# Modulation vectors: four groups' partial products folded before the one-hot matmuls

## The chip, the cores and the metric

The kernel runs on one core of a Trainium2 chip. The metric is the device time of one execution in microseconds (us). Before the change the median of three runs is 1930.26 us (1930.08 to 1930.78). The profiled execution took 1928.32 us, of which 1926.5 us lie between its first and last instruction (the span).

## The reference, cut to what matters

Two transformer blocks of two layers each run over 256 tokens of width 1024, in float32. The part that the change touches is the modulation of the second block: for each of its two layers a vector of 6144 numbers is made from one conditioning vector `c` of 1024 numbers.

```
c_act = jax.nn.silu(c)
for l in range(2):
    mod = c_act @ w_ada[l] + b_ada[l]          # (1024,) @ (1024, 6144)
    sh1, sc1, g1, sh2, sc2, g2 = split(mod, 6)
    h  = rms_norm(x, ln1_g[l]) * (1 + sc1) + sh1
    ...
```

The two `w_ada` matrices are 48 MB of float32 weights, against one row of activations. All else (feed-forward networks, gated linear attention, attention, pooling) is the same before and after.

## The kernel before, in words

**Streaming.** All weights are read once, as chunks of about 1 MB that SyncE (SP) loads into four `raw` buffers. A chunk is cut into units of 128 columns. ScalarE rounds a unit into `uhi` (line 169), VectorE makes the rest `ulo = raw - uhi` (line 170), and TensorE does three matmuls for each block of 128 rows: high by high, high by low, low by high. This splitting runs five units ahead of TensorE. A step of the stream is one unit's matmuls, or those of a few units.

**The modulation.** `ada_plan` cuts each layer's `w_ada` into 24 groups of 256 columns, and `ada_job` puts one group's 1 MB chunk into the stream. The 48 jobs stand in the first block's four feed-forward networks, twelve in each: four between its gate and up projections, eight between its down projections. A job is VectorE's: one TENSOR_SCALAR (line 641) and seven SCALAR_TENSOR_TENSORs (line 639) multiply the chunk's eight row blocks by columns of `cact` and add them up in `acc`, 128 partitions by 256. What is left is the sum over the 128 partitions. For it GpSimd (POOL) rounds `acc` into `ah` (line 648) and makes the rest `al` (line 649), and TensorE multiplies both by a one-hot matrix, a slice of `hot`: row `i` of twelve in the PSUM tile `pso` gets the column sums of group `i`, the other rows get zeros. So each group of columns costs two matmuls of 256 columns.

**When they run.** `rest()` is put off to the end of the next step (`st.lag`). From there `st.later_pe(6, pe)` counts six further steps; then the two one-hot matmuls go into `st.small`, and `unit_mm` and `unit_two` take one of them out before each row block's matmuls. After twelve groups `ada_out` copies the rows out of PSUM (line 670), turns them with two transposes (line 675) and adds the bias.

**Buffers.** `tmp` tiles share eleven buffers of a row of 272, `slot` tiles share sixteen of 4 x 272; whoever writes a reused buffer waits for its last reader. The rings of both pools run through all parts of the kernel: `acc`, `ah` and `al` are `tmp` tiles, as are the results of the feed-forward networks' evictions on VectorE (lines 716 and 728). `pso` is one PSUM buffer, which no one else uses in a feed-forward network. A scheduler orders each engine's instructions from the recorded order and from what they wait for. POOL does little else: it sets tiles to zero, issues two small loads of `gla_w2` for each mixer of the first block (line 1225) and one of the positions (line 583), and adds shifted rows in the pooling of the second block (line 1513).

Of the kernel before, what the change touches and what calls it, by code (L numbers as in the profile page):

```python
# [10 lines left out]
F32 = mybir.dt.float32  # L11
F32R = mybir.dt.float32r
# [3 lines left out]
ALU = mybir.AluOpType  # L16
# [260 lines left out]
def two_block_kernel(ctx: ExitStack, tc: tile.TileContext, I, cst, msk, out, dbg=None, stop=None):  # L277
    nc = tc.nc
    V, S, P, G = nc.vector, nc.scalar, nc.tensor, nc.gpsimd

    const = ctx.enter_context(tc.tile_pool(name="const", bufs=1))
# [24 lines left out]
    def ps_o():  # L306
        return pso.tile([128, 512], F32, name="pso", tag="pso")
# [7 lines left out]
    def tmp(n=T1, dt=F32):  # L315
        return tmp_p.tile([128, n], dt, name="tmp", tag="tmp")

    def slot(k, n, dt=F32):
        return slot_p.tile([128, k, n], dt, name="slot", tag="slot")
# [8 lines left out]
    st = Stream(nc, raw_p, un_p)  # L328
# [22 lines left out]
    identr, negr = qmt[:, 0, :], qmt[:, 1, :]  # L351
    vmt = const.tile([128, 128], F32R, name="vmt")
    ptm = const.tile([128, 256], F32R, name="ptm")
    hot = const.tile([128, 24], F32R, name="hot")
    modT = const.tile([128, 2, 48], F32, name="modT")
    mder = const.tile([128, 2, 40], F32, name="mder")

# [10 lines left out]
    def mm(ps, lhsT, rhs, start, stop):  # L368
        P.matmul(ps, lhsT=lhsT, rhs=rhs, start=start, stop=stop)  # L369
# [152 lines left out]
    def cols(dst, src, n):  # L522
        ps = ps_t()
        P.transpose(ps[:, 0:n], src[0:n, :], ident[0:n, 0:n])
        S.copy(out=dst[:, 0:n], in_=ps[:, 0:n])
# [37 lines left out]
    def set_up():  # L563
        ra, rb, rc = consts["r"]
        cols(colA, ra, 80)
        cols(colB, rb, 122)
        cols(colC, rc, 20)
        S.activation(out=bmh, in_=colA[:, A_BM:A_BM + 32], func=AF.Copy, scale=0.5)
        S.activation(out=gnh, in_=colA[:, A_GN:A_GN + 8], func=AF.Copy, scale=0.5)
        for l in range(2):  # L570
            S.activation(out=gq8[:, l:l + 1], in_=colC[:, C_QK + 2 * l:C_QK + 2 * l + 1], func=AF.Copy, scale=0.125)
        hf = tmp(24)
        G.memset(hf, 0.0)
        G.memset(hf[:, 12:13], 1.0)
        S.copy(out=hot, in_=hf)
        cth = tmp(8)
        S.activation(out=cth, in_=colC[:, C_C:C_C + 8], func=AF.Tanh, scale=0.5)
        V.scalar_tensor_tensor(out=cth, in0=cth, scalar=1.0, in1=colC[:, C_C:C_C + 8], op0=ALU.add, op1=ALU.mult)
        V.tensor_scalar(out=cact, in0=cth, scalar1=0.5, scalar2=None, op0=ALU.mult)
# [40 lines left out]
    ada = {}  # L620
# [7 lines left out]
    def ada_job():  # L628
        if not ada_q:
            return  # L630
        l, j, src = ada_q.pop(0)
        ch = Chunk(src, 8, 256)

        def fn(t):
            acc = tmp(256)

            def part(k0, k1):
                for k in range(k0, k1):
                    V.scalar_tensor_tensor(out=acc, in0=t[:, k, :], scalar=cact[:, k:k + 1], in1=acc, op0=ALU.mult, op1=ALU.add)  # L639

            V.tensor_scalar(out=acc, in0=t[:, 0, :], scalar1=cact[:, 0:1], scalar2=None, op0=ALU.mult)
            part(1, 4)

            def rest():
                part(4, 8)
                ah = tmp(256, F32R)
                al = tmp(256, F32R)
                G.tensor_copy(out=ah, in_=acc)
                G.tensor_tensor(out=al, in0=acc, in1=ah.bitcast(F32), op=ALU.subtract)
                i = j % 12  # L650

                def one(x, first, last):
                    if first:
                        ada["p"] = ps_o()
                    mm(ada["p"][0:12, 0:256], hot[:, 12 - i:24 - i], x, first, last)
                    if last:
                        st.lag(lambda: ada_out(l, j - 11))

                def pe():
                    st.small.append(lambda: one(ah, i == 0, False))  # L660
                    st.small.append(lambda: one(al, False, i == 11))
                st.later_pe(6, pe)
            st.lag(rest)

        st.job(ch, fn)

    def ada_out(l, j0):

        rows = tmp(256)
        S.copy(out=rows[0:12], in_=ada["p"][0:12, 0:256])  # L670

        def turn():
            ps = ps_t()
            for i in range(2):
                P.transpose(ps[:, 12 * i:12 * i + 12], rows[0:12, 128 * i:128 * i + 128], ident[0:12, 0:12])
            c0 = 2 * j0
            V.tensor_tensor(out=modT[:, l, c0:c0 + 24].rearrange("p (j i) -> p j i", i=2), in0=ps[:, 0:24].rearrange("p (i j) -> p j i", i=2),
                            in1=colB[:, B_AD + 48 * l + c0:B_AD + 48 * l + c0 + 24].rearrange("p (j i) -> p j i", i=2), op=ALU.add)
        st.later_pe(2, turn)
# [1060 lines left out]
    if True:  # L1740
# [14 lines left out]
        for l in range(2):  # L1755
            for part in range(3):
# [9 lines left out]
                if l == part == 0:  # L1766
                    st.after_mm(lambda: st.later_pe(6, set_up))
# [90 lines left out]
```

## Time and profile before

| | |
|---|---|
| median of three runs | 1930.26 us |
| the profiled execution, whole | 1928.32 us |
| its span | 1926.5 us |
| TensorE busy (matmul) | 1899.2 us, 99% |
| VectorE busy | 1551.7 us, 81% |
| ScalarE busy | 1078.3 us, 56% |
| GpSimd busy | 110.1 us, 6% |
| moved by DMA | 364 MB, mean 189 GB/s |

Names as the profile has them: PE is TensorE's matmuls, PEld its weight loads, DVE is VectorE, ACT is ScalarE, POOL is GpSimd, SP is SyncE. A row `out<-in` names what an instruction writes and reads, and L369 is line 369 of the kernel, the helper through which nearly all matmuls go. A PE row's duration of some 0.28 us includes the time in the pipeline; matmuls follow each other sooner, so what one costs is read from the start of one row to the start of the next. Granted TensorE clock was 0.996 of full speed (2.4 GHz) over the span.

### The profile page before, as it was taken

What the parts mean: (1) busy time and instruction counts of PE and PEld (TensorE: products, weight loads), DVE (VectorE), ACT (ScalarE), POOL (GpSimd) and SP (SyncE); (2) the same over time, 40 slices, a digit from 0 to 9 for tenths busy, and PEclk for the clock granted to TensorE, in tenths of its full rate; (3) what the DMA queues carried; (4) which work ended last, traced back from release to release, by engine and by line L of the source; (5) the groups of instructions that cost most, each with busy time, mean ns of one, the idle gap of its engine ahead of it and who ended that gap; (6) DMA issues with size and microseconds to landing.
All of it is one profiled execution on the core that took longest, in us unless ns stands there. A gap on an engine that the chain in (4) does not pass through costs nothing.

```text
span 1926.5 us, 35869 instructions
## 1 busy us (share of the span) xinstructions
PE 1899.2 (99%) x14386; PEld 1821.9 (95%) x14386; DVE 1551.7 (81%) x2932; ACT 1078.3 (56%) x1883; POOL 110.1 (6%) x146
## 2 busy tenths in 40 slices
PE   9999999999999999999999999999999999999998
PEld 8999989899999999998999999899999889999987
DVE  6978888887889887888888898986888557788854
ACT  5444456755444544456666455577676447767642
POOL 1001100000001100110000010120000002000000
PEclk9999999999999999999999999999999999999999
DMA  7767742356659766874236686944665554456551
GB/s 239 242 214 260 238 154 67 88 175 197 219 192 297 231 213 211 271 237 132 88 92 209 195 267 227 290 130 156 190 189 191 181 169 134 159 186 190 194 176 66
DMA packets 349715, 364.00 MB, mean 189 GB/s; under 512 B 6138, under 2 KB 339516, under 8 KB 349548
## 3 DMA queue, kind: packets, MB, share of 16 engines
q1 hardware_dynamic: 349372, 361.51, 58.4%
q8 instruction: 113, 1.85, 0.4%
q14 instruction: 54, 0.44, 0.1%
q0 software_dynamic: 176, 0.20, 0.0%
HBM read 360.64 MB, written 1.05 MB: 188 GB/s over the span
## 4 chain that ended last, share of the span: by engine, by line
PE 86%; DVE 7%; ACT 4%; issue 1%; DMA 1%; SPq 0%; DVEq 0%; ACTq 0%
PE big L369 38%; PE pss L369 23%; PE pst L369 20%; PE pso L369 3%; DVE ulo L170 2%; ACT uhi L169 1%; PE pst L1474 0%; PE pst L1172 0%; DMA raw<-in_w_in_dram 0%; DVE slot L928 0%; DVE tmp L639 0%; DVE tmp L1297 0%; DVE slot L1359 0%; DVE slot L926 0%; ACT tmp L1137 0%
## 5 line engine op out<-in xcount | busy, mean ns | idle before, releaser
L169 ACT CAST uhi<-raw 128x1024 fp32r<-128x1024 f32 (+3 forms) x642 | 622.3, 975 | 618.1 <-PE big L369 251.5
L170 DVE TENSOR_TENSOR ulo<-raw,uhi 128x1024 fp32r<-128x1024 f32 (+3 forms) x644 | 731.7, 1140 | 186.8 <-ACT uhi L169 179.5
L369 PE MATMUL big<-xh,uhi 128*128 128x272 f32 (+2 forms) x1560 | 453.7, 291 | 0.9 <-DVE slot L876 0.9
L369 PE MATMUL big<-xl,uhi 128*128 128x272 f32 (+2 forms) x1560 | 446.9, 286 | 0.8 <-DVE xl L1648 0.8
L369 PE MATMUL big<-xh,ulo 128*128 128x272 f32 (+2 forms) x1560 | 446.9, 286 | 0.0
L369 PEld LDWEIGHTS big<-xh,uhi 128*128 128x128 f32 x1560 | 296.2, 190 | 5.8 <-issue 4.0
L369 PEld LDWEIGHTS big<-xl,uhi 128*128 128x128 f32 x1560 | 296.3, 190 | 1.7 <-DVE xl L1648 1.0
L369 PEld LDWEIGHTS big<-xh,ulo 128*128 128x128 f32 x1560 | 296.0, 190 | 0.1
L369 PE MATMUL big<-slot,uhi 128*128 128x272 f32 (+2 forms) x1224 | 287.8, 317 | 0.0
L369 PE MATMUL big<-slot,ulo 128*128 128x256 f32 (+1 forms) x781 | 221.5, 284 | 0.5 <-DVE ulo L170 0.5
L369 PEld LDWEIGHTS big<-slot,uhi 128*128 128x128 f32 x1224 | 202.1, 189 | 16.3 <-ACT uhi L169 0.2
L369 PE MATMUL pss<-slot,uhi 128*128 128x272 f32 (+2 forms) x814 | 195.2, 319 | 0.3 <-ACT P L1460 0.3
L369 PE MATMUL pst<-xh,uhi 128*128 128x272 f32 (+2 forms) x672 | 191.5, 287 | 0.0
L369 PE MATMUL pss<-xh,uhi 128*128 128x272 f32 (+2 forms) x664 | 190.2, 289 | 0.7 <-DVE h L512 0.7
L369 PE MATMUL pst<-xh,ulo 128*128 128x272 f32 (+2 forms) x672 | 190.9, 286 | 0.0
L369 PE MATMUL pst<-xl,uhi 128*128 128x272 f32 (+2 forms) x672 | 190.7, 286 | 0.0
L369 PE MATMUL pss<-xl,uhi 128*128 128x272 f32 (+2 forms) x664 | 189.0, 287 | 0.0
L369 PE MATMUL pss<-xh,ulo 128*128 128x272 f32 (+2 forms) x664 | 188.4, 286 | 0.0
L369 PE MATMUL pst<-slot,uhi 128*128 128x272 f32 (+2 forms) x730 | 177.9, 322 | 0.0
L639 DVE SCALAR_TENSOR_TENSOR tmp<-raw,cact,tmp 128x256 f32<-128x256 f32 x336 | 164.5, 489 | 3.5
L369 PE MATMUL pss<-slot,ulo 128*128 128x256 f32 (+1 forms) x525 | 148.9, 284 | 0.0
L369 PEld LDWEIGHTS big<-slot,ulo 128*128 128x128 f32 x781 | 147.6, 189 | 0.7 <-DVE ulo L170 0.7
(451 smaller groups left out, 3209.6 us busy)
## 6 DMA issues: line engine op xcount, KB each, us to landing
raw<-in_w_ff_dram SPq DMA_DIRECT2D x64, 1024.0 KB
raw<-in_w_in_dram SPq DMA_DIRECT2D x60, 1024.0 KB
raw<-in_w_ada_dram SPq DMA_DIRECT2D x48, 1024.0 KB
raw<-in_ffn_w_up_dram SPq DMA_DIRECT2D x44, 1024.0 KB
raw<-in_ffn_w_gate_dram SPq DMA_DIRECT2D x43, 1024.0 KB
raw<-in_ffn_w_down_dram SPq DMA_DIRECT2D x32, 1024.0 KB
raw<-in_w_out_dram SPq DMA_DIRECT2D x16, 1024.0 KB
raw<-in_ffn_w_down_dram SPq DMA_DIRECT2D x16, 768.0 KB
```

The lines of the kernel that those rows point to most:

```text
L169: nc.scalar.copy(out=hi[:, k], in_=src[:, k])
L170: self.lag(lambda k=k: nc.vector.tensor_tensor(out=lo[:, k], in0=src[:, k], in1=hi[:, k].bitcast(F32), op=ALU.subtract))
L369: P.matmul(ps, lhsT=lhsT, rhs=rhs, start=start, stop=stop)
L639: V.scalar_tensor_tensor(out=acc, in0=t[:, k, :], scalar=cact[:, k:k + 1], in1=acc, op0=ALU.mult, op1=ALU.add)
```

## The change

Four jobs in a row now form a set. After each job POOL issues four DMAs, which copy the four 32-partition quarters of `acc` side by side into partitions 32q to 32q+31 of a `slot` tile `b`, where q is the job's place in its set. After the fourth job POOL adds the four quarters of `b` (two TENSOR_TENSORs, over 512 and 256 columns), so that 32 partitions are left to sum for each group, and makes `ah` and `al` of the result once for the set. `hot` has a 1 in column 8+q for the 32 rows of place q, so one pair of one-hot matmuls gives four rows of `pso`. Three pairs fill the twelve rows, where there were twelve pairs. The pair is put into `st.small` eight steps after the fourth job instead of six after every job.

```diff
-    hot = const.tile([128, 24], F32R, name="hot")
+    hot = const.tile([128, 20], F32R, name="hot")
...
-        hf = tmp(24)
+        hf = tmp(20)
         G.memset(hf, 0.0)
-        G.memset(hf[:, 12:13], 1.0)
+        for q in range(4):
+            G.memset(hf[32 * q:32 * q + 32, 8 + q:9 + q], 1.0)
...
             def rest():
                 part(4, 8)
+                q, i = j % 4, j // 4 % 3
+                if q == 0:
+                    ada["b"] = slot(4, 256)
+                b = ada["b"]
+                for a in range(4):
+                    G.dma_start(out=b[32 * q:32 * q + 32, a, :], in_=acc[32 * a:32 * a + 32])
+                if q < 3:
+                    return
                 ah = tmp(256, F32R)
                 al = tmp(256, F32R)
-                G.tensor_copy(out=ah, in_=acc)
-                G.tensor_tensor(out=al, in0=acc, in1=ah.bitcast(F32), op=ALU.subtract)
-                i = j % 12
+                G.tensor_tensor(out=b[:, 0:2, :], in0=b[:, 0:2, :], in1=b[:, 2:4, :], op=ALU.add)
+                G.tensor_tensor(out=b[:, 0, :], in0=b[:, 0, :], in1=b[:, 1, :], op=ALU.add)
+                G.tensor_copy(out=ah, in_=b[:, 0, :])
+                G.tensor_tensor(out=al, in0=b[:, 0, :], in1=ah.bitcast(F32), op=ALU.subtract)

                 def one(x, first, last):
                     if first:
                         ada["p"] = ps_o()
-                    mm(ada["p"][0:12, 0:256], hot[:, 12 - i:24 - i], x, first, last)
+                    mm(ada["p"][0:12, 0:256], hot[:, 8 - 4 * i:20 - 4 * i], x, first, last)
...
-                    st.small.append(lambda: one(al, False, i == 11))
-                st.later_pe(6, pe)
+                    st.small.append(lambda: one(al, False, i == 2))
+                st.later_pe(8, pe)
```

How the built programs differ at three places. First POOL, from the set-up of `hot` to the first mixer's loads of `gla_w2`; before, a CAST and a TENSOR_TENSOR stand there for each of the first four jobs.

```order
L573 MEMSET tmp 128x24
L574 MEMSET tmp 128x1
L648 CAST tmp<-tmp 128x256
L649 TENSOR_TENSOR tmp<-tmp 128x256
...
L1223 MEMSET slot 32x512
L1225 DMA slot<-in_gla_w_dram 16x4x64 x2
```

In the changed kernel a set of four jobs is sixteen DMAs and four instructions, two sets stand ahead of the mixer's MEMSET, and four DMAs of the third.

```order
L573 MEMSET tmp 128x20
L575 MEMSET tmp 32x1 x4
L652 DMA slot<-tmp 32x256 x16
L657 TENSOR_TENSOR slot<-slot 128x512
L658 TENSOR_TENSOR slot<-slot 128x256
L659 CAST tmp<-slot 128x256
L660 TENSOR_TENSOR tmp<-slot,tmp 128x256
...
L652 DMA slot<-tmp 32x256 x4
L1233 MEMSET slot 32x512
L1235 DMA slot<-in_gla_w_dram 16x4x64 x2
```

So the loads of `gla_w2` have moved from behind the fourth job to behind the ninth. Over the whole program POOL gets 192 of the DMAs and 12 of each of the four instructions, and loses its 48 pairs.

Second PE, in the down projections of the last feed-forward network. The names with numbers are single tiles; before, the pair of job 43 (counted from 0) stands round the first matmuls of the unit `uhi_14836`, and the next two units are `uhi_14862` and `uhi_14912`.

```order
L369 MATMUL pso_13388<-tmp_14792,hot_125 12x256 [waits Pool_49]
L369 MATMUL big_14877<-slot_13563,uhi_14836 128x512 [waits Activation_49]
L369 MATMUL big_14877<-slot_13563,ulo_14837 128x256 [waits DVE_49]
L369 MATMUL pso_13388<-tmp_14793,hot_125 12x256 [waits Pool_49]
...
L369 MATMUL big_14915<-slot_13563,uhi_14862 128x512 [waits Activation_49]
...
L369 MATMUL big_14877<-slot_14161,uhi_14912 128x512 [waits Activation_49]
```

After the change the pair of the set of jobs 40 to 43 stands round the first matmuls of the unit that was `uhi_14912` and is now `uhi_14927`.

```order
L369 MATMUL big_14893<-slot_13573,uhi_14852 128x512 [waits Activation_49]
...
L369 MATMUL big_14930<-slot_13573,uhi_14878 128x512 [waits Activation_49]
...
L369 MATMUL pso_14395<-tmp_14806,hot_125 12x256 [waits Pool_49]
L369 MATMUL big_14893<-slot_14173,uhi_14927 128x512 [waits Activation_49]
L369 MATMUL big_14893<-slot_14173,ulo_14928 128x256 [waits DVE_49]
L369 MATMUL pso_14395<-tmp_14807,hot_125 12x256 [waits Pool_49]
```

So the pair of a set's fourth job has moved two units later, here past 32 matmuls; in the eleven other sets it moves past 48. Elsewhere PE's matmuls keep their order, but for four pairs of transposes (line 675), which come about 50 matmuls later; 72 one-hot matmuls are gone (96 before, 24 after).

Third DVE, at the second job of the first feed-forward network, where an eviction's result (`tmp_915`, in the changed kernel `tmp_916`) takes over a buffer; before, it waits for PE, and the second job's first product waits for POOL.

```order
L736 TENSOR_TENSOR slot_836<-tmp_800,slot_836 128x272 [waits Activation_49]
L641 TENSOR_SCALAR tmp_910<-raw_690,cact_114 128x256 [waits DMAHW7_49,Pool_49]
L730 SCALAR_TENSOR_TENSOR tmp_876<-tmp_878,tmp_876 128x272 [waits Activation_49]
L639 SCALAR_TENSOR_TENSOR tmp_910<-raw_690,cact_114,tmp_910 128x256 [waits DVE_49]
...
L728 TENSOR_TENSOR tmp_915<-pst_880,tmp_318 128x272 [waits PE_49]
```

After the change the buffer that it takes over is the first job's `acc`.

```order
L746 TENSOR_TENSOR slot_840<-tmp_804,slot_840 128x272 [waits Activation_49]
L642 TENSOR_SCALAR tmp_911<-raw_694,cact_114 128x256 [waits DMAHW7_49]
L740 SCALAR_TENSOR_TENSOR tmp_877<-tmp_879,tmp_877 128x272 [waits Activation_49]
L640 SCALAR_TENSOR_TENSOR tmp_911<-raw_694,cact_114,tmp_911 128x256 [waits DVE_49]
...
L738 TENSOR_TENSOR tmp_916<-pst_881,tmp_318 128x272 [waits DMASW2_49,DMASW1_49,DMASW3_49,DMASW0_49,PE_49]
```

The eviction has kept its place and got a wait for the four DMAs that read that `acc`; other reuses of an `acc` buffer get the same.

## Rows read from the trace of the kernel before

**Rows 1.** The page: busy time of each engine, then the chain that ended last.

```profile
PE 1899.2 (99%) x14386; PEld 1821.9 (95%) x14386; DVE 1551.7 (81%) x2932; ACT 1078.3 (56%) x1883; POOL 110.1 (6%) x146
...
PE 86%; DVE 7%; ACT 4%; issue 1%; DMA 1%; SPq 0%; DVEq 0%; ACTq 0%
```

**Rows 2.** Waits of PE, longest first: total us, times, longest us.

```profile
PE pst L963 <- DVE slot L951: 6.0, 2, 3.7
...
PE big L369 <- DVE ulo L170: 1.2, 2, 0.8
```

**Rows 3.** Busy time by stretch: first and last feed-forward network's down projections.

```profile
120.00:230.00 110.00, 110.00 (x880) 109.33 (x880) 91.98 (x158) 51.84 (x70) 15.66 (x21) 1.00 0.80 258
...
1160.00:1255.00 95.00, 94.19 (x618) 85.50 (x617) 86.53 (x157) 48.96 (x75) 13.60 (x16) 1.00 0.83 267
```

**Rows 4.** The tile `hot`: duration ns min/median/max, first and last start.

```profile
L369 PE MATMUL pso<-tmp,hot x96: 275/281/287, 59.4 to 1253.1; 128*12 128x256 f32 x96
```

**Rows 5.** PE in order of time round one pair: start us, duration us.

```profile
167.53 0.28 PE L369 MATMUL pso<-tmp,hot 128*12 128x256 f32 x1
167.65 0.42 PE L369 MATMUL pst<-slot,uhi 128*128 128x272 f32 x2
...
168.02 0.28 PE L369 MATMUL pso<-tmp,hot 128*12 128x256 f32 x1
168.14 0.29 PE L369 MATMUL pst<-slot,uhi 128*128 128x272 f32 x1
```

**Rows 6.** POOL's instructions by line: busy us, mean ns, idle before.

```profile
L649 POOL TENSOR_TENSOR tmp<-tmp 128x256 fp32r<-128x256 f32 x48 | 45.7, 952 | 3.8
L648 POOL CAST tmp<-tmp 128x256 fp32r<-128x256 f32 x48 | 30.4, 634 | 1121.8 <-DVE tmp L639 809.6 <-PE pst L369 249.9 <-DVE xl L1272 33.1
L1225 POOL DMA_DIRECT2D slot<-in_gla_w_dram x4 | 2.2, 550 | 0.6 <-POOL slot L1223 0.6
```

**Rows 7.** Line by line: duration ns min/median/max; line 1225's DMAs, line 583's landing.

```profile
L1225 POOL DMA_DIRECT2D slot<-in_gla_w_dram x4: 512/516/658, 122.5 to 746.1; - x4
...
DMA to landing us min/median/max: 3.3/3.8/4.6
...
DMA to landing us min/median/max: 5.0/5.0/5.0
```

**Rows 8.** POOL in order of time: the CASTs of jobs 0, 7, 8 and 43.

```profile
50.70 0.40 POOL L648 CAST tmp<-tmp 128x256 fp32r<-128x256 f32 x1 [16.66 <-DVE tmp L639]
...
180.76 0.40 POOL L648 CAST tmp<-tmp 128x256 fp32r<-128x256 f32 x1 [5.16 <-DVE tmp L639]
...
191.63 0.40 POOL L648 CAST tmp<-tmp 128x256 fp32r<-128x256 f32 x1 [8.63 <-DVE tmp L639]
...
1206.76 1.30 POOL L648 CAST tmp<-tmp 128x256 fp32r<-128x256 f32 x1 [5.86 <-PE pst L369]
```

**Rows 9.** PE in order of time: first one-hot matmul of jobs 7 and 43, a later unit.

```profile
190.69 0.28 PE L369 MATMUL pso<-tmp,hot 128*12 128x256 f32 x1
...
1212.55 0.28 PE L369 MATMUL pso<-tmp,hot 128*12 128x256 f32 x1
...
1218.31 0.28 PE L369 MATMUL big<-slot,ulo 128*128 128x256 f32 x1
```

**Rows 10.** POOL and DVE in order of time, 198.2 to 199.7 us.

```profile
198.59 1.26 POOL L648 CAST tmp<-tmp 128x256 fp32r<-128x256 f32 x1 [5.75 <-DVE tmp L639]
...
198.38 1.22 DVE L170 TENSOR_TENSOR ulo<-raw,uhi 128x1024 fp32r<-128x1024 f32 x1
```

**Rows 11.** Lines 648 and 649: duration ns min/median/max.

```profile
L648 POOL CAST tmp<-tmp x48: 396/398/1321, 50.7 to 1242.2; 128x256 fp32r<-128x256 f32 x48
...
L649 POOL TENSOR_TENSOR tmp<-tmp x48: 733/746/2395, 51.2 to 1242.8; 128x256 fp32r<-128x256 f32 x48
```

**Rows 12.** DVE in order of time: the eviction that reuses the first job's `acc` after the change.

```profile
66.46 0.43 DVE L728 TENSOR_TENSOR tmp<-pst,tmp 128x272 f32<-128x272 f32 x1
```

**Rows 13.** The matmuls that read `gla_w2`'s tile: duration, first and last start.

```profile
L369 PE MATMUL pss<-tmp,slot x16: 387/388/492, 237.9 to 865.7; 32*128 32x272 f32 x16
```

## The prediction

> **What bounds the kernel now.** I read the page's busy times and the chain first. TensorE's matmuls fill 99% of the span and make 86% of the chain; no other engine is over 81% [rows 1]. Then the waits of PE, to see whether 99% hides stalls: the longest entry is 6.0 us in two waits in the mixers, and the wait that a weight-bound stream would show, for `ulo`, is 1.2 us in all [rows 2]. Third, the stretches in which the modulation runs. In the first network's down projections PE is busy for all of 110 us, DVE for 91.98 us (84%), the DMA engines for 0.80; in the last network's it is 94.19 of 95 us, 86.53 us (91%) and 0.83 [rows 3]. So in all four networks time is the sum of what PE executes, at the full clock (1.00, that is 2.4 GHz), and a matmul taken off PE is time taken off, as long as its replacement is never late.
>
> **What is removed.** 96 one-hot matmuls run now [rows 4]. What one costs is the shift of the next start: from 167.53 to 167.65 and from 168.02 to 168.14, 0.12 us each [rows 5]; read so for all 96 of [rows 4], the mean is 0.118 us. The row's own 0.28 us overlaps the next matmul and is not the price. 72 of the 96 go: 72 x 0.118 = 8.5 us. Their weight loads lie beside matmuls and give nothing more. On POOL 48 CASTs and 48 TENSOR_TENSORs go, 30.4 and 45.7 us [rows 6], none of it on the chain.
>
> **What is added on POOL, and whether PE waits for it.** The new chain of a set, from its fourth `acc` on: four DMA issues, the landing of the last one, an add over 512 columns, an add over 256, a CAST, and then PE may start. Nothing before shows a 32 KB copy from SBUF to SBUF; the nearest rows are POOL's loads of 16 KB (issue 0.550 us in the mean, landing 3.3 to 4.6 us, median 3.8) and one of 128 KB that landed in 5.0 us [rows 6, 7]. An add over 256 columns is a line 649 (0.952 us in the mean), over 512 I take two of them, and the CAST is a line 648 (0.634 us) [rows 6]. By these: 4 x 0.550 + 3.8 + 1.9 + 0.95 + 0.63 = 9.5 us. I take that, the means being of the same engine under the same load. The lower end, by minima and medians: 4 x 0.512 + 3.3 + 1.5 + 0.75 + 0.40 = 8.0 us. The upper end, everything at its worst: issues of 0.658 us that each also wait out one VectorE instruction of 1.22 us (why, below), landing 5.0, adds at 2.395, CAST 1.321 [rows 7, 10, 11]: 4 x 1.88 + 5.0 + 4.8 + 2.4 + 1.3 = 21.0 us.
>
> Against this stands the time that PE leaves. Job 7's `acc` is ready at 180.76, where its CAST starts [rows 8], and its first one-hot matmul starts at 190.69 [rows 9]: 9.9 us; the pair now comes 48 matmuls later, at 0.125 us each 6.0 us, so 15.9 us are left. The same sum for all twelve sets gives 15.8 to 18.3 us, but for one: job 43's CAST starts at 1206.76, its matmul at 1212.55, and the last of the 32 matmuls that it is moved past starts at 1218.31 [rows 8, 9], which leaves 11.3 us once the 0.24 us of the old pair is taken off. The twelve add up to 198 us. At 9.5 us no set waits; at 13 us only the tight one does, by 1.7 us. I put the wait at 0.
>
> **Why POOL's times scatter.** POOL's CAST takes 0.40 us or 1.26 us. The long one at 198.59 ends at 199.85, and beside it DVE's `ulo` runs from 198.38 to 199.60 at its usual 1.22 us [rows 10, 11]: POOL stood still until DVE was through, and DVE lost nothing. The Trainium skill says so too, in "SBUF — State Buffer", section "Who interferes with whom": a VectorE instruction with two SBUF inputs contends with a GpSimd instruction that reads SBUF, and whoever comes first holds the port. By that rule the issues might be spared, since the page infers that making descriptors needs the write side; by its box on DMAs that DVE blocks (section "SBUF: two separate sides") they starve while DVE runs a two-port mode. The first would leave the sum as it is; the second is a rival below. The loads at 122.5 and 745.6 us bear out the first as far as four of them can.
>
> **What else is moved.** `acc` is now held until four DMAs have read it. The eviction that takes over job 0's buffer starts at 66.46 [rows 12], `acc` is ready at 50.70 [rows 8]: 15.8 us for 4 x 0.550 + 3.8 = 6.0 us (at worst 12.5). Behind that eviction DVE's queue holds the next splits, but it is not reached. `ah` and `al` are held two steps longer, but by three pairs in twelve jobs instead of twelve. `b` is a `slot` tile held for four jobs; a network takes eleven of the sixteen, so with its three `b` fourteen. The two loads of `gla_w2` are moved behind job 8's four issues, ready at 191.63 [rows 8]: they land near 200 us, and the first reader is at 237.9 [rows 13]. The DMA engines get 6.3 MB more on 364; in a down projection that is 1 MB on some 24, and 0.80 to 0.83 [rows 3] becomes 0.83 to 0.86. SP's queue is as it was. Each costs 0 as long as those margins stand; were the loads late, PE would wait in the first splits after a late chunk.
>
> **The sum.** The profiled execution took 1928.32 us, its span 1926.5. Minus 8.5 us is 1919.8 for such an execution. The median of the runs is 1.94 us above the profiled execution, so 1930.26 - 8.5 = 1921.8 us.
>
> **Rivals.**
> - *The small copies come late and PE waits (slower).* Place: the first one-hot matmul of a set, which blocks PE's queue. It costs the chain's excess over each set's 11.3 to 18.3 us; the gain is gone at a chain of some 16.7 us, 7 us over my 9.5. One way there: the copies stand behind weight chunks in the DMA engines. A chunk of 1 MB takes 4.06 us at 258 GB/s [rows 3]; behind two of them the chain is 17.6 us and the twelve sets wait 15.1 us in all: 1936.9 us. Were each issue starved to the upper end of 21.0 us, it would be 12 x 21.0 - 198 = 54 us and 1976 us. For it speaks that DMA is busiest just where eight of twelve jobs run. Against it: POOL's loads landed in 3.3 to 5.0 us while weights streamed [rows 7]. "DMA: Bandwidth & Descriptors" of the Trainium skill, section "Queues, rings and completion order", has each DMA engine take turns between queues packet by packet, and by that rule the copies wait for packets, not for chunks. Chance 0.08.
> - *PE's time is filled again (no change).* If VectorE or the weights set the pace in the down projections, the eight sets there give nothing: two thirds of the matmuls, 48 x 0.118 = 5.7 us, are lost, the rest stays, and 1927.5 us comes out, within the bound. DVE's 91% in the last network speaks for it; against it, PE has next to no waits there [rows 2, 3], and DVE's own work stays the same. Chance 0.12.
> - *My forecast*, with at most the tight set waiting: 1919.5 to 1926. Chance 0.80.
>
> **How the numbers follow.** 0.2% of the time, about what a measurement of this kernel can tell from no change, is 3.9 us, so "faster" begins below 1926.4 and "slower" above 1934.1. The forecast is wholly in the first; the second rival in the middle; the first rival splits, 0.02 with a few us of waits in the middle and 0.06 above. So 0.80, 0.14, 0.06. The range runs from 1919.5, where some small wait goes with the removed matmuls, to 1928, which takes in the second rival's number; what is left out is the first rival and a little of the second.
>
> **What would show it.** In the changed kernel's profile: 24 one-hot matmuls at the same 0.12 us; a PE waits list without POOL in it; the networks shorter by about 2.1 us each (18 matmuls), the mixers and the second block unchanged; 192 small copies landing in under 6 us; POOL's chain of a set done within 11 us. Wrong would be: a wait of PE for POOL in several sets, DVE evictions waiting for small copies, or PE waits for `uhi` or `ulo` in the down projections.

## The result, and the profile after

The changed kernel takes 1949.58 us (1946.61 to 1954.4, 4 runs) against 1930.17 us for the kernel before on the same chip: a ratio of 1.0103, 95% interval 1.0079 to 1.0128. It is 19.4 us slower, where 8.5 us of gain were forecast, and it lies outside the forecast's range. The profiled execution is the slowest of the four (1954.4 us, span 1952.6, 26.1 over the one of before), so what follows is read from the traces for places and causes, and from the ratios for sizes.

The page's busy times, against [rows 1]:

```profile
PE 1910.2 (98%) x14314; PEld 1831.4 (94%) x14314; DVE 1552.7 (80%) x2932; ACT 1077.3 (55%) x1883; POOL 177.5 (9%) x293
```

TensorE runs 72 matmuls fewer and is busy 11 us longer. The tile `hot` and line 652, the small copies (duration ns min/median/max; first and last start; landing of the copies), show what was added and removed just as written, against [rows 4, 7]:

```profile
L369 PE MATMUL pso<-tmp,hot x24: 277/280/284, 139.8 to 1284.9; 128*12 128x256 f32 x24
...
L652 POOL DMA_DIRECT2D slot<-tmp x192: 496/496/636, 53.1 to 1269.1; - x192
...
DMA to landing us min/median/max: 3.5/5.4/7.5
```

The waits of PE (us in total, times, longest) have no POOL in them. What is new against [rows 2] is short: waits for pieces that VectorE and ScalarE make, of the weights (`ulo`) and of the next matmuls' input (`xl`, `xh`).

```profile
PE pst L973 <- DVE slot L961: 6.0, 2, 3.7
PE big L369 <- DVE ulo L170: 4.5, 4, 2.5
PE pss L369 <- DVE xl L456: 3.6, 4, 1.0
...
PE pss L369 <- ACT xh L451: 2.9, 4, 1.5
```

They stand where a feed-forward network ends. Three slices of 10 us there (busy us and instructions of PE, PEld, DVE, ACT, POOL; granted clock; DMA share; GB/s), first before, then after:

```profile
210.00:220.00 10.00, 10.00 (x83) 9.94 (x82) 9.69 (x16) 4.99 (x6) 2.01 (x3) 1.00 0.79 249
220.00:230.00 10.00, 10.00 (x80) 9.85 (x80) 4.74 (x8) 6.83 (x9) 0.00 (x0) 1.00 1.03 321
230.00:240.00 10.00, 9.95 (x71) 8.87 (x71) 9.70 (x20) 4.72 (x7) 0.00 (x0) 1.00 0.20 68
```

```profile
210.00:220.00 10.00, 9.88 (x80) 9.66 (x79) 9.96 (x20) 4.18 (x6) 1.96 (x4) 1.00 0.75 230
220.00:230.00 10.00, 6.32 (x38) 5.47 (x37) 6.15 (x11) 4.83 (x8) 3.87 (x6) 0.85 1.10 338
230.00:240.00 10.00, 10.00 (x65) 9.77 (x65) 7.83 (x14) 6.63 (x7) 3.25 (x3) 0.80 0.82 260
```

Before, 80 matmuls start between 220 and 230 us; after, 38. TensorE stands still for 3.7 us of these ten, and behind that its granted clock is 0.85 and 0.80, that is, for a part of the slice it is at 1.2 instead of 2.4 GHz. The clock is how a short stall grows: over the span the mean granted clock is 0.984 after and 0.996 before, 31.2 - 7.7 = 23.5 us of full clock not granted. In the other three executions of the changed kernel the mean is 0.987 to 0.988.

ScalarE's waits for loaded weights, before and then after, are four times as long:

```profile
ACT uhi L169 <- DMA raw<-in_ffn_w_down_dram: 22.0, 10, 3.4
```

```profile
ACT uhi L169 <- DMA raw<-in_ffn_w_down_dram: 87.1, 27, 5.9
```

Where the time goes by stage: the start of the ScalarE logarithm behind each of the four networks (227.3, 647.7, 850.0 and 1251.6 us before) and at their beginnings gives how much longer each network is than before, in one profiled execution of each kernel.

| kernel | network 1 | 2 | 3 | 4 | sum |
|---|---|---|---|---|---|
| changed kernel | +4.9 | +4.5 | +8.1 | -0.1 | +17.4 |
| e15, removal alone | -1.9 | -2.1 | -1.5 | -0.8 | -6.3 |
| e11, removal and fold, old order | -0.7 | -0.1 | +1.4 | +0.7 | +1.3 |
| e10, removal and fold, new order | +3.3 | +1.7 | +1.1 | -2.5 | +3.6 |
| e8, the change in the old order | +0.5 | -1.9 | +0.2 | +8.2 | +7.0 |
| e12, copies of constants at other times, new order | +4.0 | +5.3 | +5.5 | +3.3 | +18.1 |

Most of the rest of the changed kernel's loss falls in the two mixers that follow a network (5.9 and 2.8 us); other kernels show up to 5.6 us there with the clock low near 270 and 320 us, so the mixers are partly the clock's chance.

### The profile page after: what moved, and what is told of

The parts are those of the page before. It is cut to its first block, busy times and chain, and to the rows that moved or that the text cites. A ratio compares the mean times of both kernels' runs of the same rounds, so it can differ in the third digit from the quotient of the medians.

```text
span 1952.6 us, 35985 instructions
## 1 busy us (share of the span) xinstructions
PE 1910.2 (98%) x14314; PEld 1831.4 (94%) x14314; DVE 1552.7 (80%) x2932; ACT 1077.3 (55%) x1883; POOL 177.5 (9%) x293
## 4 chain that ended last, share of the span: by engine, by line
PE 56%; DVE 5%; ACT 3%; DMA 1%; issue 1%; DVEq 0%; ACTq 0%
PE big L369 25%; PE pss L369 15%; PE pst L369 13%; DVE ulo L170 2%; PE pso L369 1%; ACT uhi L169 1%; DMA raw<-in_ffn_w_down_dram 1%; DMA raw<-in_w_in_dram 1%; DVE tmp L640 0%; PE pst L1484 0%; DVE slot L1369 0%; DVE tmp L1307 0%; DVE slot L1384 0%; PE pst L1182 0%; DVE slot L1526 0%
## 5 line engine op out<-in xcount | busy, mean ns | idle before, releaser
L652 POOL DMA_DIRECT2D slot<-tmp x192 | 94.6, 499 | 1023.0 <-DVE tmp L640 534.7
```

The lines of the kernel that those rows point to most:

```text
L652: G.dma_start(out=b[32 * q:32 * q + 32, a, :], in_=acc[32 * a:32 * a + 32])
```

## The experiments

"Old order" means the order in which VectorE's and ScalarE's instructions stand in the kernel before, "new order" that of the changed kernel. The scheduler chooses it, and the change made it choose another: SP's order is equal, VectorE's differs in all four networks. A kernel is "held" to an order by edges that only fix the issue order and wait for nothing (the call is shortened here):

```diff
+    for a, b in zip(to, to[1:]):
+        tc.add_manual_dep(es[b], es[a].name, NoSync, reason="issue order")
```

Where nothing else is said of 24 one-hot sums, they are due 8 steps on, as in the change; 96 are due 6 steps on, as before. "Other times" are explained under e4 and e12.

Ratios to the kernel before on the same chip, with 95% intervals, and the us over before that they make on 1930 us:

| run | one-hots | transfers | fold | order | ratio | us |
|---|---|---|---|---|---|---|
| changed kernel | 24 | of acc | POOL | new | 1.0103 (1.0079 to 1.0128) | +19.9 |
| e1 | 24, due 6 | none | none | nearly old | 0.9979 (0.9969 to 0.9989) | -4.1 |
| e2 | 96 | of acc, unread | none | its own | 1.0126 (1.0108 to 1.0143) | +24.3 |
| e3 | 24 | POOL copies | POOL | nearly new | 1.0069 (1.0054 to 1.0084) | +13.3 |
| e4 | 96 | of constants, other times | none | nearly old | 1.0011 (1.0000 to 1.0021) | +2.1 |
| e5 | 24, due 6 | of acc | POOL | old | 1.0147 (1.0133 to 1.0161) | +28.4 |
| e6 | 24, due 6 | POOL copies | POOL | old | 1.0017 (1.0006 to 1.0027) | +3.3 |
| e7 | 96 | none | none | that of e2 | 1.0042 (1.0029 to 1.0054) | +8.1 |
| e8 | 24 | of acc | POOL | old | 1.0056 (1.0044 to 1.0069) | +10.8 |
| e9 | 96 | of constants, 384, other times | none | old | 1.0120 (1.0102 to 1.0138) | +23.2 |
| e10 | 24 | none | POOL | new | 1.0001 (0.9991 to 1.0011) | +0.2 |
| e11 | 24 | none | POOL | old | 1.0006 (0.9998 to 1.0015) | +1.2 |
| e12 | 24 | of constants, other times | POOL | new | 1.0119 (1.0104 to 1.0134) | +23.0 |
| e13 | 24 | of acc, last set POOL copies | POOL | old | 1.0029 (1.0018 to 1.0041) | +5.6 |
| e14 | 24, due 6 | none | none | old | 0.9969 (0.9959 to 0.9980) | -6.0 |
| e15 | 24 | none | none | old | 0.9972 (0.9962 to 0.9982) | -5.4 |
| e16 | 24, due 6 | none | POOL | old | 1.0018 (1.0007 to 1.0029) | +3.5 |
| e17 | 24 | POOL copies | adds on VectorE | old | 1.0087 (1.0073 to 1.0100) | +16.8 |

**e1: the removal alone.**

```diff
-                    st.small.append(lambda: one(ah, i == 0, False))
+                    st.small.append(lambda: one(ah, i == 3, False))
...
-                st.later_pe(6, pe)
+                if i % 4 == 3:
+                    st.later_pe(6, pe)
```

> The kernel before, with three of every four pairs of one-hot sums left out (its modulation is then made of a quarter of the weights); POOL's casts stay, there are no copies and no fold, and VectorE and ScalarE keep nearly the order of before. All theories expect the gain that the prediction had from the removal, 72 x 0.118 = 8.5 us, so about 1921.7 us. If it stays at 1930, the removal is worth nothing and that step of the prediction fails too.

It gained 4.1 us, half of the 8.5; all theories missed by as much.

**e2: the copies alone, unread.** Four `G.dma_start` of `acc` ahead of the two casts; nothing reads `b`.

> The kernel before with its 96 one-hot sums, and the 192 small copies of acc added, into a tile that nothing reads. The changed kernel lost 19.4 us where 8.5 us of gain were forecast, so a full loss is about 28 us. Theory T (the copies' traffic holds up the weight loads): about 1958 us. Theory O (with the copies the scheduler puts the instructions of VectorE and ScalarE into another order, which splits the weights later): about 1958 us too, since the order of this kernel differs from that of before nearly as much as the changed kernel's does. Theory H (the accumulators are held until the copies have landed, and the tile pool runs short): about 1958 us as well. If none of the copies matters and the fold is at fault, 1930.

It lost 24 us. All three theories allow that. Its list of waits is not that of the changed kernel: PE waits for POOL's CAST, which now comes behind the four issues, and VectorE waits for the small copies.

```profile
PE pso L369 <- POOL tmp L654: 6.0, 3, 4.2
...
DVE tmp L722 <- DMA slot<-tmp: 4.4, 2, 3.0
```

**e3: POOL copies instead of transfers.**

```diff
-                    G.dma_start(out=b[32 * q:32 * q + 32, a, :], in_=acc[32 * a:32 * a + 32])
+                    G.tensor_copy(out=b[32 * q:32 * q + 32, a, :], in_=acc[32 * a:32 * a + 32])
```

> The changed kernel with each of the 192 small transfers done by a POOL copy of 32x256 instead of a DMA; everything else of the change stays, TensorE's order is the same, and VectorE's is nearly that of the changed kernel. Theory T: with the transfers gone the loss goes, about 1921.7 us. Theory O: the order stays, so the loss stays, about 1949 us. Theory H: the accumulators come free after some 2 us instead of 5 to 8, so about 1921.7 us.

Between the two: a third of the loss goes with the transfers, 13.3 us stay without them. Theories T and H, each by itself, fall, since both expected the whole loss to go.

**e4: as many copies, of constants, in nearly the old order.** `in_=cs[32 * a:32 * a + 32, 0:256]`, behind the casts.

> The kernel before, with 192 transfers of the same size and from the same queue behind POOL's two casts of each job, but read from a table of constants instead of acc, into a tile that nothing reads. VectorE and ScalarE keep nearly the order of before and no accumulator is held longer. Theory T: the traffic is there, so about 1958 us. Theory O and theory H: neither the order nor the holding has changed, so about 1930 us.

It lost 2.1 us. But this is not the traffic of the change at the times of the change: a copy of constants waits for no job, and POOL issued them early and in bursts. In the first network the first and the last issues are these:

```profile
36.44 4.07 POOL L655 DMA_DIRECT2D slot<-cs  x8 [0.15 <-issue]
...
165.78 1.54 POOL L655 DMA_DIRECT2D slot<-cs  x3 [1.83 <-DMA slot<-cs]
```

In the changed kernel half of the network's copies come later than that, the last ones at 220.58:

```profile
220.58 1.96 POOL L652 DMA_DIRECT2D slot<-tmp  x4 [3.29 <-DVE tmp L640]
```

So e4 shows that 192 such copies can cost almost nothing. It does not show whether that is due to the order or to the times, and the terms of 2.1 us in later expectations rest on it.

**e5, e6, e7: the order held.**

> The changed kernel (its one-hot sums due 6 steps on, as before, not 8), with the instructions of VectorE and ScalarE held to the order in which they stand in the kernel before, by ordering edges that wait for nothing. Transfers, fold and 24 one-hot sums are those of the change. Theory O (the order is what costs; the traffic of the copies cost 2.1 us in e4, the removal gave 4.1 to 4.7 in e1): 1931 - 4.4 + 2.1, about 1929 us. Theory H (the accumulators are held until the copies land, which stands here as in the changed kernel): about 1949 us. Theory T (traffic first): near 1944, since only a part of the loss was gone in e3 without the transfers.

> e3 (POOL copies instead of transfers), held to the order of before in the same way. Theory O: removal alone is left, 1931 - 4.4, about 1926.5 us, faster than both kernels. Rival P (in e3 POOL's 192 copies and VectorE hold each other up, since POOL is busy 245 us there and 117 in e1): the loss of e3 stays, about 1944 us. Theory H: 1926.5 too, as POOL has read the accumulators some 2 us after they are made.

> The kernel before, with nothing added and nothing removed; only VectorE and ScalarE are held to the order in which their instructions stand in e2 (which had the unread copies and took 1954). Theory O: the order alone costs what e2 lost beyond the 2.1 us of traffic that e4 showed, 24.3 - 2.1 = about 22, so 1953 us; by e3 (13.3 lost and 4.4 gained) some 17, so 1948. If the order costs nothing without the transfers: 1931, and what e2 lost is the transfers' doing.

e5 missed all three numbers, by a fault of its making: it had the sums due after 6 steps, and in the waits of PE the prediction's first rival stands:

```profile
PE pso L369 <- POOL tmp L659: 21.6, 8, 5.3
```

Chains of about 10 us do not fit into 6 steps. e6 shows that POOL copies, without a landing, do, and that 10 of e3's 13.3 us go with the order; the gain of 4.4 is missing in it, which e16 takes up. e7 shows that an order can cost by itself, 8 us of the 17 to 22 expected. Against e2, which has the same order of VectorE and ScalarE, it also shows what copies at the times of the jobs cost without a fold: 24.3 - 8.1 = 16 us, the waits listed under e2 among them.

**e8 to e11: transfers and order, one at a time, sums due 8 steps on.** e10 and e11 leave out the transfers:

```diff
-                for a in range(4):
-                    G.dma_start(out=b[32 * q:32 * q + 32, a, :], in_=acc[32 * a:32 * a + 32])
                 if q < 3:
                     return
+                G.tensor_copy(out=b[:, 0, :], in_=acc)
+                G.memset(b[:, 1:4, :], 0.0)
```

> The changed kernel just as it is, one-hot sums due 8 steps on, with VectorE and ScalarE held to the order of before (the four modulation transposes' copies and additions left free). In e5 the sums were due after 6 steps and TensorE waited 21.6 us for POOL in 8 waits; that is mended here. Two causes, order and traffic: if the order makes most of the loss (e3 without transfers lost 13.3 in the new order, e6 2.9 in the old one, 10.4 apart), this takes about 1949 - 10.4 = 1939 us; if traffic and order only add up from e1 and e4 (-4.4 and +2.1), 1928. If the transfers alone make it, whatever the order: 1949.

> e4 with its 192 unread transfers of constants made 384 (8 behind each job, into two tiles), VectorE and ScalarE held to the order of before, all one-hot sums kept. If the traffic costs in proportion: twice the 2.1 us of e4, about 1934.5 us. If the DMA engines have room for one such load and not for two, since their share in the down projections is over 0.8 already: 1940 or more. If the traffic costs nothing and e4 was chance: 1930.

> The changed kernel without its 192 transfers (the fold takes the last group's accumulator and zeros in their place, so three quarters of the modulation are left out), held to VectorE's and ScalarE's order of the changed kernel. If the order costs by itself: about 10 above e11, 1937 us or, by e3, up to 1944. If the order only costs together with the transfers: 1926, the same as e11.

> The same as e10, without transfers, held to the order of before. Only the removal of 72 one-hot sums is left: 1926 us by e1 (4.1 to 4.7 gained), 1921.7 by the prediction's 8.5 us.

With the changed kernel this is a table of four: without transfers +0.2 (new order) and +1.2 (old), with them +19.9 and +10.8. So in sum the new order costs nothing by itself and 9 us together with transfers; the transfers cost 10 us in the old order and 20 in the new; and with neither, the gain is not there. The nothing is a balance: by the table of stages e10 is 4.0 us slower than e11 in network 1, 1.8 in network 2, and 3.2 faster in network 4. In e8's profile 8.2 us are lost in network 4 alone, where PE waited for POOL once:

```profile
PE pso L369 <- POOL tmp L659: 4.2, 1, 4.2
```

That is the set of jobs 44 to 47, not the tight one of the prediction. e9 cost 23 us, far more than in proportion, but it is not clean: beside 8 issues of 0.5 us a job, POOL waited 68.7 us for earlier copies to land, its casts came late, and PE waited 8.8 + 5.2 us for lines 648 and 649. Its copies, too, are not issued at the times of the change.

**e12, e13: traffic or holding, and the last set.**

> The changed kernel in its own order of VectorE and ScalarE, with its 192 transfers read from a table of constants instead of the accumulators (a POOL copy of one column of the accumulator paces them; the modulation is then wrong and is not used for anything else). The traffic is that of the change, the accumulators are free as soon as VectorE has made them. If it is the traffic that lengthens the loads in this order: about 1949 us, as the changed kernel. If it is that the accumulators are held until the copies have landed: about 1931, as e10 without transfers.

> e8 (the change in the old order, 11.2 us over before), with the last set's 16 transfers done by POOL copies. In e8 TensorE waited 4.2 us for POOL once, in the last set, and the granted clock fell behind it (0.80, 0.85 and 0.83 in three slices of 10 us: 5.2 us). If that wait is e8's loss, 1941.7 - 4.2 - 5.2, about 1932 us, and transfers cost little in the old order, as in e4. If the transfers cost in every network, as in the changed kernel, about 1940.

e12 lost as much as the changed kernel, with the accumulators free, so theory H is not needed for a loss of this size; and in the changed kernel no wait of VectorE or ScalarE for a small copy is listed. But the pacing failed. Only the first four copies of a set waited for a job, and the other twelve followed at once; in the first set, shown here, the fold's first add ran before the second job was ready:

```profile
51.57 1.74 POOL L652 COPY slot<-tmp 128x1 f32<-128x1 f32 x1 [16.82 <-DVE tmp L640]
53.25 4.08 POOL L654 DMA_DIRECT2D slot<-cs  x8
...
67.63 1.28 POOL L659 TENSOR_TENSOR slot<-slot 128x512 f32<-128x512 f32 x1 [4.31 <-DMA slot<-cs]
...
72.83 1.47 POOL L652 COPY slot<-tmp 128x1 f32<-128x1 f32 x1 [3.04 <-DVE tmp L640]
```

So the transfers cost in this order at these times too, spread over the networks in another way (+3.3 us in network 4, where the changed kernel loses nothing); that the two sums agree may be chance.

e13 halves e8's loss, 5.6 us instead of 10.8: the last set's wait made about 5, the other transfers some 4 over e11.

**e14, e15, e16: what the removal is worth.**

> e1 (the kernel before with 72 of its 96 one-hot sums left out), held to exactly the order of before. e1 gained 4.1 to 4.7 us, e11 nothing. If the removal is worth what e1 showed: 1926 us. If the time comes back at the ends of the networks, where TensorE then waits for the weights, as in e11: 1930 to 1932. By the prediction's step: 1921.7.

> e14 (72 one-hot sums left out, order of before, 5.9 us gained) with the remaining sums due 8 steps on instead of 6. e11, with the same order on TensorE, VectorE and ScalarE, POOL's casts once a set and its fold, gained nothing. If the due of 8 is what took the gain away in e11: about 1930 to 1932. If it is POOL's fold: about 1924, as e14.

> e11 (no transfers, fold and casts once a set, order of before) with its sums due 6 steps on. The other half of the same question: about 1924 if the due of 8 took the gain, 1930 to 1932 if POOL's fold did.

The due does not matter: 6.0 and 5.4 us of gain without POOL's fold, 3.5 and 1.2 us of loss with it, whichever the due. e11 and e15 have the same order on TensorE and nearly the same on VectorE and ScalarE; they differ in POOL's work. VectorE's busy time, with the same 2932 instructions, is 1559.1 us in e11 and 1550.6 in e15. e11 and e16 also have, once a set, a POOL copy and a MEMSET that the change does not have.

**e17: the adds on VectorE.** A whole version: e3 with `V.tensor_tensor` for the two adds, held to the old order.

> A whole version without transfers: POOL copies in place of the 192 transfers, the two adds of each fold on VectorE instead of POOL, sums due 8 steps on, the rest held to the order of before. By the runs so far: 5.7 gained by the removal (e14, e15), the POOL copies cost nothing (e6 against e16, both 2.9 to 3.0 over before), POOL's fold cost about 7 (e11 against e15). If it is POOL's adds beside VectorE that cost: VectorE gets 12 x about 1 us of adds, much of it in the networks where its share is over 0.9, so about 1924 to 1930 us, at best faster than both kernels. If the fold costs wherever it is done: 1932 to 1934.

16.8 us slower, beyond every number expected. A wait of VectorE in it:

```profile
DVE bsum L657 <- POOL bsum L652: 17.9, 12, 1.8
```

12 x (0.69 + 0.42) = 13.3 us of adds and 17.9 us of queueing behind POOL's copies: 31 us taken from VectorE went with 16.8 + 5.4 = 22 us of time. No whole version beat the kernel before.

## Why the prediction was wrong, step by step

**"A matmul taken off PE is time taken off."** Two thirds right. Alone, the removal gave 5.4 to 6.0 us of 8.5 (e14, e15), spread over the networks as forecast but with 1.6 us each instead of 2.1. Where the rest went is not settled: e15 shows no wait of PE at a network's end, but ScalarE waits 44.2 us for down-projection weights in it, twice as long as before, so TensorE has caught up with the stream.

**"DVE lost nothing."** This step failed. Rows 10 showed a one-input CAST of POOL that stood still beside VectorE, and I carried that over to the fold. The trace of before held the other case already, line 649, which has two inputs, beside a `ulo` of 1024 columns that took 1.81 us instead of its usual 1.22 [rows 10]:

```profile
192.11 0.74 POOL L649 TENSOR_TENSOR tmp<-tmp 128x256 fp32r<-128x256 f32 x1
...
192.12 1.81 DVE L170 TENSOR_TENSOR ulo<-raw,uhi 128x1024 fp32r<-128x1024 f32 x1 [0.36 <-ACT uhi L169]
```

POOL's adds have two inputs too, and they held VectorE. POOL and VectorE of the changed kernel in the first network:

```profile
188.75 2.01 POOL L657 TENSOR_TENSOR slot<-slot 128x512 f32<-128x512 f32 x1 [6.03 <-DMA slot<-tmp]
190.84 0.81 POOL L658 TENSOR_TENSOR slot<-slot 128x256 f32<-128x256 f32 x1
...
192.28 0.80 POOL L660 TENSOR_TENSOR tmp<-slot,tmp 128x256 fp32r<-128x256 f32 x1
...
188.64 0.96 DVE L170 TENSOR_TENSOR ulo<-raw,uhi 128x768 fp32r<-128x768 f32 x1 [1.75 <-ACT uhi L169]
189.52 1.52 DVE L640 SCALAR_TENSOR_TENSOR tmp<-raw,cact,tmp 128x256 f32<-128x256 f32 x1
190.96 0.98 DVE L456 SCALAR_TENSOR_TENSOR xl<-h,colN,xh 128x272 fp32r<-128x272 f32 x1
...
192.40 0.97 DVE L459 TENSOR_TENSOR tmp<-tmp 128x272 f32<-128x272 f32 x1
...
193.69 0.34 DVE L642 TENSOR_SCALAR tmp<-raw,cact 128x256 f32<-128x256 f32 x1
```

The same instructions in e10, same order, where POOL had its fold done by 186.4:

```profile
187.83 0.96 DVE L170 TENSOR_TENSOR ulo<-raw,uhi 128x768 fp32r<-128x768 f32 x1 [0.19 <-ACT uhi L169]
188.71 0.48 DVE L640 SCALAR_TENSOR_TENSOR tmp<-raw,cact,tmp 128x256 f32<-128x256 f32 x1
189.10 0.50 DVE L456 SCALAR_TENSOR_TENSOR xl<-h,colN,xh 128x272 fp32r<-128x272 f32 x1
...
189.91 0.43 DVE L459 TENSOR_TENSOR tmp<-tmp 128x272 f32<-128x272 f32 x1
...
190.66 0.34 DVE L642 TENSOR_SCALAR tmp<-raw,cact 128x256 f32<-128x256 f32 x1
```

0.48 became 1.52, 0.50 became 0.98, 0.43 became 0.97; with the 0.81 us that the first `ulo` came later, line 642 is 3.03 us late. The port rule that the prediction took from "SBUF — State Buffer" ("Who interferes with whom", the Trainium skill) has whoever comes first hold the port; this trace agrees, in the direction that I left out. By e11 against e15 the fold in place of the 48 casts costs about 6.6 us.

That the fold costs this by holding VectorE is argued and not shown. POOL's two-input work has not grown: it was 48 x 256 columns and is 12 x (512 + 256 + 256), the same number, in longer stretches and at other places. And VectorE's busy time in sum does not go with the time: it is 1551.7 us before and 1552.7 in the changed kernel; 1544.7 in e10 and 1559.1 in e11, which take the same time; 1559.7 in e16 and 1575.7 in e6, which has the 192 POOL copies besides, and these two again take the same time. What a hold costs depends on where it falls.

**"Were the loads late, PE would wait ..."**, priced at 0. This step failed too, and it is the largest error: the transfers cost 10 us in the old order and 20 in the new (e8 against e11, the changed kernel against e10). How they cost it was read at one place. The 3.03 us run on through VectorE to the `ulo` of 768 columns, whose end frees a weight buffer; SP issues the next load 0.03 us behind it. SP, then ScalarE's cast of a later chunk, of the changed kernel, then of e10:

```profile
197.31 0.37 SPq L149 DMA_DIRECT2D raw<-in_w_ada_dram  x1
...
201.67 2.00 ACT L169 CAST uhi<-raw 128x1024 fp32r<-128x1024 f32 x2 [5.83 <-DMA raw<-in_ffn_w_down_dram]
```

```profile
194.28 0.37 SPq L149 DMA_DIRECT2D raw<-in_w_ada_dram  x1
...
198.44 2.00 ACT L169 CAST uhi<-raw 128x1024 fp32r<-128x1024 f32 x2 [3.64 <-DMA raw<-in_ffn_w_down_dram]
```

3.03 us late at the issue, 3.23 at the cast. "SP's queue is as it was" holds for its order and fails for its times: the stream is a ring of four buffers that VectorE frees, so a late split makes a late load and a late load a late split. ScalarE waited 22.0 us for down-projection weights before, 48.7 in e10 and 48.8 in e8, 80.1 in e12 and 87.1 in the changed kernel: the two kernels with transfers and the new order stand apart, as they do in time. Below that the wait does not sort the kernels: it is 44.2 us in e15, the fastest but one, 41.0 in e17, which lost 16.8, and 57.4 in e13, which lost 5.6. The transfers may act in two ways that this place shows together: the loads land later beside them (of the 0.81 us here 0.4 stand already in the loads' issue, so 0.4 us), and the fold must wait for a landing, 6.03 us here, which moved it from e10's place to one where VectorE was behind. How the 10 and 20 us divide between the two is not settled; the 16 us between e2 and e7, which have no fold, say that the second is not needed for a large loss.

**The order.** A step that is missing from the prediction. It took VectorE's queue as given; the scheduler gave the changed kernel another one. Alone that cost nothing in sum (e10, e11), with transfers 9 us, with POOL copies 10 (e3, e6, which differ in the due as well), and another order cost 8 alone (e7). Why this order bears late loads less well was only read from the trace (in it the next job's multiplications stand ahead of the 768-column `ulo`), and not tried.

**POOL's chain.** Right in mechanism, a little long: 180.76, the last issue, to 192.20, the end of the CAST, is 11.4 us instead of 9.5, by the landing (6.03 us here, 5.4 in the median, instead of 3.8); the issues took 1.96 us instead of 2.2 and the first add 2.01 instead of 1.9. No set made PE wait. That margin was the order's gift: in the old order the last set was 4.2 us late (e8).

**The rivals.** The second, that VectorE or the weights set the pace, had a chance of 0.12 and comes nearest to what the traces show, with a wrong end: it was held to give back at most the eight sets' gain, since "DVE's own work stays the same". A pace that another engine sets can also get slower, and then the loss has no such floor. The first, that PE waits because the copies come late, did not happen in the changed kernel and did in e5 and e8, by 21.6 and 4.2 us.

**The account**, by the ratios: removal -5.4 (e15), fold instead of casts +6.6 (e11), transfers in the old order +9.6 (e8, about half of it the last set's wait), the new order with them +9.1; together +19.9. The four are differences along one path of runs, so they add up by their making; on a path over e10 the fold and the new order together get +5.6 and the transfers +19.7.

## What to carry to other kernels

An engine at 99% is not the only bound when the stream that feeds it has no slack: find the ring that feeds it, and ask where an added microsecond falls on the engines that free its buffers: 16 us more on VectorE cost nothing in e6, and 3 us at one place of the changed kernel made a load 3 us late. Before trusting a diff, compare the issue order of every engine before and after, since a scheduler may change the queues that the prediction takes as given. Work on an idle engine is not free where it makes another engine's instructions longer, and a trace of before can show that, if one looks at every form and not at one row. Before using a stand-in for traffic, check in its trace that it runs at the same times.

## What the runs showed of the hardware that was not expected

- A copy of 32 KB from SBUF to SBUF, issued by POOL, took 3.5 to 7.5 us from issue to landing, median 5.4; from a table of constants the median was 5.4 too (e4). The 16 KB loads from memory of [rows 7] landed in 3.3 to 4.6; behind the small copies the same loads took 6.2 in the median.
- POOL's instructions with two inputs made the VectorE instruction beside them two to three times as long: 1.52 us instead of 0.48 beside an add of 128x512, 0.98 instead of 0.50 and 0.97 instead of 0.43 beside instructions of 128x256. With its 192 one-input copies of 32x256 VectorE was busy 16.0 us longer (e6 against e16), and the kernel's time did not change (1.0017 and 1.0018).
- Where TensorE stood still for 3.7 us at the end of the first network (changed kernel), the slices of 10 us show a granted clock of 0.85 and then 0.80; after 4.6 us at the end of the fourth in e8, 0.80 and 0.85; after 1.2 us at the end of the first in e11 it stayed at 1.00.
